# Hybrid attention layer on one core: the first norm's weights as one row spread by TensorE, and FoX value weights in row blocks

## The chip, the cores and the metric

The kernel runs on one NeuronCore of a Trainium2 chip. Its engines are TensorE (PE, with its weight loads listed apart as PEld), VectorE (DVE), ScalarE (ACT), GpSimd (POOL) and SyncE (SP), which issues most of the transfers. Each engine works through its own list of instructions in a fixed order. The metric is device time in microseconds (us) of one execution.

## The reference

The layer takes x (1024 tokens by 1024 channels, float32). It normalizes x, projects it, runs two attentions on the projections (a dilated sliding-window one and a forgetting one, "FoX"), merges them by sigmoid gates, adds the result to x, and then applies a second norm and a SwiGLU feed-forward part. The change lies in the first norm and in the FoX values:

```python
h = rms_norm(x, norm_mix_g[layer])           # x * rsqrt(mean(x*x) + 1e-6) * g
proj = h @ w_in[layer]
fox = proj[..., o2:o3].reshape(b, s, 3, N_FOX_HEADS, HEAD_DIM)
...
o_b = forgetting_attention(fox[:, :, 0], fox[:, :, 1], fox[:, :, 2],
                           jax.nn.log_sigmoid(f_logit))
```

`fox[:, :, 2]`, the values, are 512 columns of `proj`: 1024 tokens by 512, each a sum over the 1024 channels.

## The kernel before, in words

Every large product is made of three matmuls. `split` (lines 98 to 100) cuts a float32 operand into a rounded part `hi` (an ACT copy, line 99) and a rest `lo` (a DVE subtraction, line 100), and `mm3` (lines 102 to 105) adds hi·hi, hi·lo and lo·hi in one PSUM bank. So each weight tile costs ACT one pass and DVE one pass before TensorE can use it.

The kernel's first stage, the pool `foxv` from line 398 on, normalizes the eight blocks of 128 tokens and computes the FoX values. `norm_transpose` (lines 167 to 182) treats one block: ACT squares and sums it (line 171), `rstd` (lines 145 to 165) makes the factor with two small ACT operations (`t` on line 157 and `y` on line 158) and four small DVE ones, DVE multiplies by the factor and by the norm's weights `gain1` (line 173), and TensorE transposes the result `hn` in two groups of four 128x128 tiles (line 178), which `split` moves to `hT`. `values(i)` then multiplies block i of `hT` by the value weights `wv`.

What stands ahead of that is written out by hand. SP issues, in this order, the first block of x (`xt`, line 405), the norm's 1024 weights written to all 128 partitions (line 409), and then `wv` in four blocks of 128 columns with all 1024 rows (line 122, in `load_w`), the later blocks of x among them. TensorE starts with 20 matmuls of a constant tile `ones` whose result nobody reads (`dummies`, line 422), and later six more. The callback `between`, here `first_tokens`, puts the norm of block 0 between the splits of the first and second weight block, and the norm of block 1 between the second and third; `tc.issue_after(ins)` tells the scheduler to place what follows behind `ins` on the same engine, in order of issue only. Since a block of 128 columns serves only its own columns, `values` computes tokens of blocks 0 and 1 in two halves of 256 columns: the first half needs two weight blocks, and the second half the other two. From block 2 on it takes all 512 columns at once.

The rest of the layer follows in stages of its own: the dilated values, query and key projections, the two attentions, the gates, the output product and the feed-forward part. The scheduler chooses the order of instructions on each engine from the dependencies and from the `issue_after` edges.

Of the kernel before, what the change touches and what calls it, by code (L numbers as in the profile page):

```python
# [8 lines left out]
F32 = mybir.dt.float32  # L9
# [6 lines left out]
P = 128  # L16
D = 1024
# [30 lines left out]
def layer_kernel(  # L48
# [42 lines left out]
    def nm(s):  # L91
        uid[0] += 1
        return f"{s}_{uid[0]}"
# [11 lines left out]
        last_mm[0] = nc.tensor.matmul(psum, w.lo, m.hi, start=False, stop=stop)  # L105

    last_mm, last_hi, last_sq = [None], [None], [None]
    last_w, s12_hi = [None], [None]

    def load_w(src, kt, n, tag="w", bufs=2, pool=None, chunk=None, rpool=None, rbufs=2, shared=0, between=None):  # L110

        pool = pool or wpool
        row = -(-n // P) * P
        hi = pool.tile([P, kt, row], F32R, tag=tag + "h", name=nm("wh"), bufs=bufs)
        lo = pool.tile([P, kt, row], F32R, tag=tag + "l", name=nm("wl"), bufs=bufs)
        chunk = chunk or n
        for c0 in range(0, n, chunk):
            cs = slice(c0, min(n, c0 + chunk))
            own = rpool and c0 >= shared
            raw = (rpool if own else wpool).tile([P, kt, cs.stop - c0], F32, tag="wr", name=nm("wr"),  # L120
                                                 bufs=rbufs if own else 2)
            last_w[0] = nc.sync.dma_start(out=raw[:], in_=src[:, cs].rearrange("(k p) c -> p k c", p=P))
            if between and 0 < c0 <= 2 * chunk:
                between(c0 // chunk)

            with tc.issue_after((last_hi, last_sq)[c0 // chunk - 1][0].ins) if between and 0 < c0 <= 2 * chunk \
                    else ExitStack():
                split(hi[:, :, cs], lo[:, :, cs], raw[:])
        return Pair(hi, lo)


# [13 lines left out]
    def rstd(ss, by_sqrt):  # L145

        def tiny(n):
            return small.tile([P, 1], F32, tag=n, name=nm(n))

        y, t, v, r = tiny("y"), tiny("t"), tiny("v"), tiny("r")  # L150
        nc.vector.tensor_scalar(out=v[:], in0=ss[:], scalar1=1.0 / D, scalar2=EPS,
                                op0=ALU.mult, op1=ALU.add)
        if by_sqrt:
            nc.scalar.activation(out=t[:], in_=ss[:], func=AF.Sqrt, scale=1.0 / D, bias=epst[:])
            nc.vector.reciprocal(out=y[:], in_=t[:])
        else:
            nc.scalar.activation(out=t[:], in_=ss[:], func=AF.Ln, scale=1.0 / D, bias=epst[:])
            nc.scalar.activation(out=y[:], in_=t[:], func=AF.Exp, scale=-0.5)
        t2 = tiny("t2")
        nc.vector.tensor_scalar(out=t2[:], in0=y[:], scalar1=v[:, 0:1], scalar2=y[:, 0:1],  # L160
                                op0=ALU.mult, op1=ALU.mult)
        nc.vector.tensor_scalar(out=t2[:], in0=t2[:], scalar1=-0.5, scalar2=1.5,
                                op0=ALU.mult, op1=ALU.add)
        nc.vector.tensor_scalar(out=r[:], in0=y[:], scalar1=t2[:, 0:1], scalar2=None, op0=ALU.mult)
        return r

    def norm_transpose(xt, gain, hT, col, pool, by_sqrt, bufs=2):
# [2 lines left out]
        ss = small.tile([P, 1], F32, tag="ss", name=nm("ss"))  # L170
        last_sq[0] = nc.scalar.activation(out=hn[:], in_=xt, func=AF.Square, accum_out=ss[:])
        r = rstd(ss, by_sqrt)
        nc.vector.scalar_tensor_tensor(out=hn[:], in0=xt, scalar=r[:, 0:1], in1=gain[:],  # L173
                                       op0=ALU.mult, op1=ALU.mult)
        for k0 in range(0, KT, 4):
            pt = psf.tile([P, HALF], F32, tag="f", name=nm("pt"))
            for k in range(4):
# [220 lines left out]
    with pool_of("foxv", 2) as vpool:  # L398
# [7 lines left out]

        load_x()
        gain1 = vpool.tile([P, D], F32, tag="gain", name=nm("gain"), bufs=1)
        nc.sync.dma_start(out=gain1[:], in_=norm_mix_g.broadcast_to([P, D]))
        nc.gpsimd.memset(ones[:], 1.0)  # L410

        warm = pd()
# [7 lines left out]
        def dummies(n):  # L420
            for i in range(n):
                nc.tensor.matmul(warm[:, :P], ones[:], ones[:], start=True, stop=True)

        def first_tokens(n):
            if n == 1:
                load_x()
                norm_transpose(xts[0][:], gain1, hT[0], 0, vpool, False)
                dummies(6)
            else:
                with tc.issue_after(last_hi[0].ins):  # L430
                    norm_transpose(xts[1][:], gain1, hT[0], P, vpool, False)

        dummies(20)
        wv = load_w(w_in[:, FOX0 + 2 * FOX_W:FGT0], KT, FOX_W, tag="wv", bufs=1, pool=vpool,
                    chunk=P, rpool=vpool, rbufs=3, shared=2 * P, between=first_tokens)

        def values(i):
            hh, c = divmod(i * P, HALF)
            st = vpool.tile([P, FOX_W], F32, tag="vst", name=nm("vst"), bufs=2)
            n = 256 if i < 2 else FOX_W  # L440
            for c0 in range(0, FOX_W, n):
                pv = pd()
                for k in range(KT):
                    mm3(pv[:, :n], hT[hh][:, k, c:c + P], wv[:, k, c0:c0 + n], k == 0, k == KT - 1)
                nc.vector.tensor_copy(st[:, c0:c0 + n], pv[:, :n])
            nc.gpsimd.dma_start(out=vf_dram[i], in_=st[:])

        for i in range(NT):
# [893 lines left out]
```

## Time and profile before

| | |
|---|---|
| median of 3 runs | 1468.48 us (1467.93 to 1469.89) |
| the profiled execution | 1468.82 us, of which the span is 1467.1 us |
| busy share of the span: PE, PEld, DVE, ACT, POOL | 98%, 79%, 65%, 38%, 34% |
| PE busy in the first 20 us | 14.41 us |
| PE busy from 40 to 60 us | 20.00 us |

The span runs from the first to the last instruction that the profile counts; 1.7 us of the execution's own time lie around it. In the profile's rows a time stands at the start in us from the beginning of the span, then the duration, the engine, the line of the kernel, the operation, and output and input by the program's names. `[... <-X]` tells how long the engine was idle before the row and what ended that. A matmul's duration is modelled and overlaps the next one's, so the distance between two starts is what a matmul costs in a row of them.

### The profile page before, as it was taken

Reading aid. Unit: us, or ns where it says so; the run is one execution under the profiler, and the core shown is the slowest. Engines: PE = TensorE matmul, PEld = TensorE weight load, DVE = VectorE, ACT = ScalarE, POOL = GpSimd, SP = SyncE. Lnnn points to the kernel's source line nnn. Section 1 sums busy time; section 2 is a strip of 40 time slices with the busy share of each in tenths; the row PEclk is TensorE's granted clock in tenths of the full one; section 3 lists DMA queues with packets and bytes.
Section 4 is the critical chain, followed back from the end, with each engine's and each line's share of the span. In section 5 each row is a group of like instructions: output and inputs, shape, how many; then the busy total and the mean of one; then the engine's idle time right before and its main releaser. Section 6 shows DMA issues by size and latency. Waiting matters only on the chain. (4 is left out here: it accounts for less than half of the span.)

```text
span 1467.1 us, 18389 instructions
## 1 busy us (share of the span) xinstructions
PE 1441.3 (98%) x6876; PEld 1162.5 (79%) x6876; DVE 956.6 (65%) x1336; ACT 553.3 (38%) x824; POOL 504.1 (34%) x438
## 2 busy tenths in 40 slices
PE   8999999999999999999999999999999999999997
PEld 7898888877677776788887778888888887788886
DVE  6484654359889999846528865555556555876555
ACT  5333332236656423354315432223223323543333
POOL 1020444535533321110146166666666665000000
PEclk9999999999999999999999999999999999999999
DMA  7232454575543461265759312323233332986502
GB/s 231 72 101 79 144 166 124 139 212 130 129 122 102 168 206 36 80 233 170 293 201 367 106 58 80 107 93 104 98 108 108 107 103 88 384 287 210 164 29 86
DMA packets 165785, 213.58 MB, mean 146 GB/s; under 512 B 13760, under 2 KB 115136, under 8 KB 165440
## 3 DMA queue, kind: packets, MB, share of 16 engines
q1 hardware_dynamic: 129376, 119.06, 26.2%
q0 software_dynamic: 15344, 55.59, 10.4%
q10 hardware_dynamic: 20976, 37.76, 8.2%
q8 instruction: 54, 0.88, 0.3%
q14 instruction: 35, 0.29, 0.1%
HBM read 146.32 MB, written 66.06 MB: 145 GB/s over the span
## 5 line engine op out<-in xcount | busy, mean ns | idle before, releaser
L299 PE MATMUL pd<-hT_t,wh 128*128 128x512 f32 x856 | 265.0, 390 | 1.4 <-DVE sg L1037 0.6
L299 PE MATMUL pd<-tT,wh 128*128 128x512 f32 x768 | 235.1, 389 | 0.7 <-ACT wh L99 0.6
L100 DVE TENSOR_TENSOR wl<-wr,wh 128x1024 fp32r<-128x1024 f32 (+2 forms) x110 | 131.2, 1194 | 127.9 <-ACT wh L99 127.3
L99 ACT ACTIVATE wh<-wr 128x1024 fp32r<-128x1024 f32 (+2 forms) x110 | 95.4, 867 | 285.6 <-PE pd L299 166.2
L299 PEld LDWEIGHTS pd<-hT_t,wh 128*128 128x128 f32 x856 | 160.0, 188 | 37.8 <-DVE sg L1037 4.7
L299 PEld LDWEIGHTS pd<-tT,wh 128*128 128x128 f32 x768 | 144.0, 188 | 31.4 <-ACT wh L99 1.0
L299 PE MATMUL pd<-hT_t,wl 128*128 128x512 f32 x428 | 166.5, 389 | 0.0
L299 PE MATMUL pd<-tT,wl 128*128 128x512 f32 x384 | 147.6, 389 | 0.0
L105 PE MATMUL pf<-hT_t,wl 128*128 128x512 f32 x288 | 114.5, 398 | 0.0
L103 PE MATMUL pf<-hT_t,wh 128*128 128x512 f32 x288 | 114.1, 396 | 0.0
L104 PE MATMUL pf<-hT_t,wh 128*128 128x512 f32 x288 | 113.7, 395 | 0.0
L100 DVE TENSOR_TENSOR ol<-raw,oh 128x1024 fp32r<-128x1024 f32 x66 | 79.6, 1223 | 45.8 <-ACT oh L99 38.5
L99 ACT ACTIVATE wh<-s 128x1024 fp32r<-128x1024 f32 x58 | 61.4, 1060 | 118.3 <-POOL s L286 91.3
L285 POOL TENSOR_TENSOR s<-wr 128x512 f32<-128x512 f32 x29 | 60.4, 2084 | 123.9 <-DMA wr<-in_w_in_dram 71.0
L99 ACT ACTIVATE oh<-raw 128x1024 fp32r<-128x1024 f32 x66 | 69.2, 1060 | 87.4 <-PE pd L1257 66.8
L299 PEld LDWEIGHTS pd<-hT_t,wl 128*128 128x128 f32 x428 | 80.3, 188 | 16.9
L100 DVE TENSOR_TENSOR wl<-s,wh 128x1024 fp32r<-128x1024 f32 x58 | 72.2, 1246 | 32.3 <-ACT wh L99 32.3
L1257 PE MATMUL pd<-ol,oh 128*128 128x512 f32 x224 | 87.2, 390 | 1.7 <-DVE ol L100 1.7
L1257 PE MATMUL pd<-oh,ol 128*128 128x512 f32 x224 | 86.3, 389 | 0.0
L984 POOL TENSOR_TENSOR r<-r 128x512 f32<-128x512 f32 x32 | 44.2, 1391 | 120.7 <-DMA r<-in_w_ffn_down_dram 119.3
L299 PEld LDWEIGHTS pd<-tT,wl 128*128 128x128 f32 x384 | 72.1, 188 | 15.0
L1257 PE MATMUL pd<-oh 128*128 128x512 f32 x224 | 83.9, 389 | 0.0
(277 smaller groups left out, 3068.4 us busy)
## 6 DMA issues: line engine op xcount, KB each, us to landing
wr<-in_w_in_dram SPq DMA_DIRECT2D x46, 512.0 KB, 4.7
wr<-in_w_ffn_in_dram SPq DMA_DIRECT2D x44, 512.0 KB, 3.8
raw<-left_dram SPq DMA_DIRECT2D x56, 256.0 KB, 5.3
g_dram<-fst ACTq DMA_DIRECT2D x32, 256.0 KB, 2.5
land<-g_dram SPq DMA_DIRECT2D x16, 512.0 KB, 3.4
r<-in_w_ffn_down_dram SPq DMA_DIRECT2D x8, 1024.0 KB, 10.4
right_dram<-r POOLq DMA_DIRECT2D x8, 1024.0 KB, 6.2
left_dram<-f POOLq DMA_DIRECT2D x8, 1024.0 KB, 4.7
```

The lines of the kernel that those rows point to most:

```text
L99: last_hi[0] = nc.scalar.activation(out=hi, in_=src, func=AF.Copy)
L100: return nc.vector.tensor_tensor(out=lo, in0=src, in1=hi.bitcast(F32), op=ALU.subtract)
L103: nc.tensor.matmul(psum, w.hi, m.hi, start=start, stop=False)
L104: nc.tensor.matmul(psum, w.hi, m.lo, start=False, stop=False)
L105: last_mm[0] = nc.tensor.matmul(psum, w.lo, m.hi, start=False, stop=stop)
L285: nc.gpsimd.tensor_tensor(out=s12[:, :4], in0=u1, in1=u2, op=ALU.add)
L299: last_mm[0] = nc.tensor.matmul(bank[:], p, q, start=first and k == 0 and n == 0, stop=k == 3 and n == 2, skip_group_check=True)
L984: nc.gpsimd.tensor_tensor(out=out, in0=p, in1=q, op=ALU.subtract)
L1257: nc.tensor.matmul(bank[:], p, q, start=new and n == 0 and i == 0, stop=n == last and i == 2, skip_group_check=True)
```

## The change

The norm's weights now come as one row of 1024 numbers to partition 0, in place of a copy for each partition. TensorE spreads them: two matmuls multiply a row of ones by 512 weights each, ACT copies the first half from PSUM to `gain1`, and DVE the second half. The first norm is placed behind these two copies on ACT and on DVE.

The value weights are loaded and split in four blocks of 256 rows (two tiles of 128 channels) and all 512 columns, in place of four blocks of 128 columns. `values` therefore takes all 512 columns at once for every token block. The order of the first splits is told by hand: block 0 behind `y` (ACT) and `hn` (DVE) of the first norm, block 1 behind the last ACT copy of the first `hT`, block 2 behind the square of the second norm, and block 3 behind the ACT half of block 2's split.

```diff
-        nc.sync.dma_start(out=gain1[:], in_=norm_mix_g.broadcast_to([P, D]))
+        nc.sync.dma_start(out=gain1[0:1, :], in_=norm_mix_g)
...
         def first_tokens(n):
+            if n == 0:
+                with tc.issue_after(spread[0]), tc.issue_after(spread[1]):
+                    norm_transpose(xts[0][:], gain1, hT[0], 0, vpool, False)
+                first_hi.append(last_hi[0].ins)
+                dummies(6)
+                return last_y[0].ins, last_hn[0].ins
             if n == 1:
                 load_x()
-                norm_transpose(xts[0][:], gain1, hT[0], 0, vpool, False)
-                dummies(6)
-            else:
+                return first_hi
+            if n == 2:
                 with tc.issue_after(last_hi[0].ins):
                     norm_transpose(xts[1][:], gain1, hT[0], P, vpool, False)
+                return [last_sq[0].ins]
+            return [last_hi[0].ins]
 
         dummies(20)
-        wv = load_w(w_in[:, FOX0 + 2 * FOX_W:FGT0], KT, FOX_W, tag="wv", bufs=1, pool=vpool,
-                    chunk=P, rpool=vpool, rbufs=3, shared=2 * P, between=first_tokens)
+        spread, first_hi = [], []
+        for c in (slice(0, HALF), slice(HALF, D)):
+            pg = pd()
+            nc.tensor.matmul(pg[:], ones[0:1, :], gain1[0:1, c], start=True, stop=True)
+            if c.start == 0:
+                spread.append(nc.scalar.activation(out=gain1[:, c], in_=pg[:], func=AF.Copy).ins)
+            else:
+                spread.append(nc.vector.tensor_copy(gain1[:, c], pg[:]).ins)
+        wv = Pair(*[vpool.tile([P, KT, FOX_W], F32R, tag="wv" + n, name=nm("wv"), bufs=1) for n in "hl"])
+        for n in range(KT // 2):
+            raw = (vpool if n > 1 else wpool).tile([P, 2, FOX_W], F32, tag="wr", name=nm("wr"), bufs=2)
+            last_w[0] = nc.sync.dma_start(out=raw[:], in_=w_in[2 * n * P:2 * (n + 1) * P, FOX0 + 2 * FOX_W:FGT0].rearrange(
+                "(k p) c -> p k c", p=P))
+            with ExitStack() as behind:
+                for ins in first_tokens(n):
+                    behind.enter_context(tc.issue_after(ins))
+                split(wv.hi[:, 2 * n:2 * n + 2], wv.lo[:, 2 * n:2 * n + 2], raw[:])
 
         def values(i):
             hh, c = divmod(i * P, HALF)
             st = vpool.tile([P, FOX_W], F32, tag="vst", name=nm("vst"), bufs=2)
-            n = 256 if i < 2 else FOX_W
-            for c0 in range(0, FOX_W, n):
-                pv = pd()
-                for k in range(KT):
-                    mm3(pv[:, :n], hT[hh][:, k, c:c + P], wv[:, k, c0:c0 + n], k == 0, k == KT - 1)
-                nc.vector.tensor_copy(st[:, c0:c0 + n], pv[:, :n])
+            pv = pd()
+            for k in range(KT):
+                mm3(pv[:], hT[hh][:, k, c:c + P], wv[:, k], k == 0, k == KT - 1)
+            nc.vector.tensor_copy(st[:], pv[:])
             nc.gpsimd.dma_start(out=vf_dram[i], in_=st[:])
```

The order of the instructions shows where the new ones stand. Line numbers in the rows of the changed kernel are its own (line 409 is the dummies, 158 the square, 165 the transposes). The first place is the start of TensorE's list; `pd_110` is the bank of the dummies, and `pt_161` and `pt_168` are the transposed halves of token block 0. Before:

```order
L422 MATMUL pd_110<-ones 128x128 x23
L178 MATMUL pt_161<-ident,hn_146 128x128 x4
L178 MATMUL pt_168<-ident,hn_146 128x128 x4
L422 MATMUL pd_110<-ones 128x128 x3
L103 MATMUL pd_225<-wh_136,hT_t 128x256
L104 MATMUL pd_225<-wl_137,hT_t 128x256
```

The same place in TensorE's list of the changed kernel:

```order
L409 MATMUL pd_110<-ones 128x128 x20
L431 MATMUL pd_136<-gain_107,ones 128x512
L431 MATMUL pd_139<-gain_107,ones 128x512
L409 MATMUL pd_110<-ones 128x128 x6
L165 MATMUL pt_161<-ident,hn_146 128x128 x4
L165 MATMUL pt_168<-ident,hn_146 128x128 x4
L103 MATMUL pd_231<-wv_142,hT_t 128x512
```

The two spreading matmuls stand behind the first 20 dummies, and all 26 dummies stand ahead of the transposes.

The second place is the start of ACT's list. `xt_105`, `xt_144` and `xt_220` are the token blocks 0, 1 and 2, and `wh_136<-wr_...` are the ACT halves of the four weight splits. Before:

```order
L171 ACTIVATE hn_146,ss_147<-xt_105 128x1024
L157 ACTIVATE t_150<-ss_147,epst 128x1
L158 ACTIVATE y_149<-t_150 128x1
L99 ACTIVATE wh_136<-wr_138 128x8x128
L99 ACTIVATE hT_t<-pt_161 128x4x128
L99 ACTIVATE hT_t<-pt_168 128x4x128
L99 ACTIVATE wh_136<-wr_142 128x8x128
L171 ACTIVATE hn_185,ss_186<-xt_144 128x1024
L99 ACTIVATE wh_136<-wr_183 128x8x128
L99 ACTIVATE wh_136<-wr_216 128x8x128
L157 ACTIVATE t_189<-ss_186,epst 128x1
L171 ACTIVATE hn_280,ss_281<-xt_220 128x1024
```

The same place in ACT's list of the changed kernel, where the token blocks 1 and 2 are called `xt_185` and `xt_226`:

```order
L433 ACTIVATE gain_107<-pd_136 128x512
L158 ACTIVATE hn_146,ss_147<-xt_105 128x1024
L144 ACTIVATE t_150<-ss_147,epst 128x1
L145 ACTIVATE y_149<-t_150 128x1
L99 ACTIVATE wv_142<-wr_144 128x1024
L99 ACTIVATE hT_t<-pt_161 128x4x128
L99 ACTIVATE hT_t<-pt_168 128x4x128
L99 ACTIVATE wv_142<-wr_183 128x1024
L158 ACTIVATE hn_191,ss_192<-xt_185 128x1024
L99 ACTIVATE wv_142<-wr_189 128x1024
L99 ACTIVATE wv_142<-wr_222 128x1024
L158 ACTIVATE hn_260,ss_261<-xt_226 128x1024
```

ACT's first instruction is now the copy of a spreading matmul's result, and the square of token block 0 stands behind it. The first small operation of block 1 (`t_189` before) no longer stands ahead of the square of block 2; it follows behind these rows.

The third place is DVE's list at the norms of blocks 1 and 2, where `vst` is the copy of finished values and `hT_t<-pt_200` (before) and `hT_t<-pt_206` (now) the DVE half of block 1's split after the transposes. Before:

```order
L164 TENSOR_SCALAR r_191<-y_188,t_25_195 128x1
L162 TENSOR_SCALAR t_41_290<-t_41_290 128x1
L173 SCALAR_TENSOR_TENSOR hn_185<-xt_144,r_191,gain_107 128x1024
L164 TENSOR_SCALAR r_286<-y_283,t_41_290 128x1
L445 COPY vst_224<-pd_225 128x256
L173 SCALAR_TENSOR_TENSOR hn_280<-xt_220,r_286,gain_107 128x1024
L445 COPY vst_224<-pd_251 128x256
L100 TENSOR_TENSOR hT_t<-pt_200,hT_t 128x4x128
L100 TENSOR_TENSOR hT_t<-pt_207,hT_t 128x4x128
```

The same place in the changed kernel:

```order
L151 TENSOR_SCALAR r_197<-y_194,t_27_201 128x1
L151 TENSOR_SCALAR r_266<-y_263,t_42_270 128x1
L160 SCALAR_TENSOR_TENSOR hn_191<-xt_185,r_197,gain_107 128x1024
L160 SCALAR_TENSOR_TENSOR hn_260<-xt_226,r_266,gain_107 128x1024
L452 COPY vst_230<-pd_231 128x512
L100 TENSOR_TENSOR hT_t<-pt_206,hT_t 128x4x128
L100 TENSOR_TENSOR hT_t<-pt_213,hT_t 128x4x128
```

Both factors (`r_`) now stand ahead of block 1's multiplication, and the values' copy, once two halves around block 2's multiplication, is one piece behind it. Block 1's split stands behind all of these in both kernels.

More of the change, by code (lines that the diff above doesn't have):

```diff
@@ L107, in layer_kernel, with load_w @@
     last_mm, last_hi, last_sq = [None], [None], [None]
[L108 to L128, printed above, removed]
+    last_w, s12_hi, last_y, last_hn = [None], [None], [None], [None]
+    def load_w(src, kt, n, tag="w", pool=None):
+        hi, lo = [(pool or wpool).tile([P, kt, -(-n // P) * P], F32R, tag=tag + h, name=nm("w" + h), bufs=2) for h in "hl"]
+        raw = wpool.tile([P, kt, n], F32, tag="wr", name=nm("wr"), bufs=2)
+        last_w[0] = nc.sync.dma_start(out=raw[:], in_=src.rearrange("(k p) c -> p k c", p=P))
+        split(hi[:], lo[:], raw[:])
         return Pair(hi, lo)
@@ L157, in rstd @@
             nc.scalar.activation(out=t[:], in_=ss[:], func=AF.Ln, scale=1.0 / D, bias=epst[:])
-            nc.scalar.activation(out=y[:], in_=t[:], func=AF.Exp, scale=-0.5)
+            last_y[0] = nc.scalar.activation(out=y[:], in_=t[:], func=AF.Exp, scale=-0.5)
         t2 = tiny("t2")
@@ L172, in norm_transpose @@
         r = rstd(ss, by_sqrt)
-        nc.vector.scalar_tensor_tensor(out=hn[:], in0=xt, scalar=r[:, 0:1], in1=gain[:],
-                                       op0=ALU.mult, op1=ALU.mult)
+        last_hn[0] = nc.vector.scalar_tensor_tensor(out=hn[:], in0=xt, scalar=r[:, 0:1], in1=gain[:],
+                                                    op0=ALU.mult, op1=ALU.mult)
         for k0 in range(0, KT, 4):
```

## The prediction

> **What bounds the kernel now.** The page comes first: TensorE is busy 98% of the span, no other engine above 79%.
>
> ```profile
> span 1467.1 us, 18389 instructions
> PE 1441.3 (98%) x6876; PEld 1162.5 (79%) x6876; DVE 956.6 (65%) x1336; ACT 553.3 (38%) x824; POOL 504.1 (34%) x438
> ```
>
> The change touches only the start, so the busy times by stretches come next (PE first after the stretch's length, the granted clock third from the end).
>
> ```profile
> 0.00:20.00 20.00, 14.41 (x95) 13.52 (x96) 9.77 (x19) 11.26 (x19) 3.48 (x13) 0.98 0.99 271
> 20.00:40.00 20.00, 19.75 (x127) 17.85 (x127) 14.94 (x30) 8.89 (x20) 1.83 (x3) 0.94 0.48 155
> 40.00:60.00 20.00, 20.00 (x101) 16.67 (x101) 13.19 (x23) 8.74 (x18) 1.63 (x3) 1.00 0.33 103
> ```
>
> TensorE sits idle for 5.6 us in the first 20 and hardly after that. So the question is when it begins the third token block's values, the first matmuls that both kernels have in the same form: what that moment moves, the end moves too, since TensorE paces what follows. The timeline gives the way there.
>
> ```profile
> 1.39 7.33 PE L422 MATMUL pd<-ones 128*128 128x128 f32 x46 [1.39 <-POOL ones L410]
> 4.67 1.06 ACT L171 ACTIVATE hn<-xt 128x1024 f32<-128x1024 f32 x1 [2.60 <-DMA xt<-in_x_dram]
> 7.23 1.28 DVE L173 SCALAR_TENSOR_TENSOR hn<-xt,r,gain 128x1024 f32<-128x1024 f32 x1
> 8.15 1.06 ACT L99 ACTIVATE wh<-wr 128x1024 fp32r<-128x1024 f32 x1 [1.71 <-DMA wr<-in_w_in_dram]
> 8.66 1.06 PE L178 MATMUL pt<-ident,hn 128*128 128x128 f32 x8
> 9.32 1.09 ACT L99 ACTIVATE hT_t<-pt 128x512 fp32r<-128x512 f32 x2
> 11.11 1.06 ACT L99 ACTIVATE wh<-wr 128x1024 fp32r<-128x1024 f32 x1 [0.70 <-DMA wr<-in_w_in_dram]
> 12.21 0.38 PE L103 MATMUL pd<-wh,hT_t 128*128 128x256 f32 x1 [1.82 <-ACT wh L99]
> 14.23 1.06 ACT L99 ACTIVATE wh<-wr 128x1024 fp32r<-128x1024 f32 x1 [0.61 <-DMA wr<-in_w_in_dram]
> 16.00 1.06 ACT L99 ACTIVATE wh<-wr 128x1024 fp32r<-128x1024 f32 x1 [0.71 <-DMA wr<-in_w_in_dram]
> 22.72 1.04 PE L178 MATMUL pt<-ident,hn 128*128 128x128 f32 x8
> 25.15 0.36 PE L105 MATMUL pd<-wh,hT_t 128*128 128x256 f32 x1
> 30.93 0.40 PE L103 MATMUL pd<-wh,hT_t 128*128 128x512 f32 x1
> 31.17 0.40 PE L104 MATMUL pd<-wl,hT_t 128*128 128x512 f32 x1
> 31.40 0.39 PE L105 MATMUL pd<-wh,hT_t 128*128 128x512 f32 x1
> ```
>
> The square of token block 0 starts when x lands (4.67). The values of block 0 do not start with the first norm: its `hT` is there from 10.4 (9.32 + 1.09), and TensorE waits until 12.21 for the second weight block, whose split waited for its landing until 11.11. The transposes of block 1 follow at 22.72, the first matmul that needs the `lo` half of its `hT` runs at 25.15, and block 2's values begin at 30.93. From 25.15 on TensorE does not stop. The start is thus bound by landings first, and then by the splits.
>
> **The change part by part.** *The spread weights, the largest term.* ACT's first instruction is now the copy of the first spreading matmul, and the square of block 0 is queued behind it; so is all of ACT's list. On TensorE that matmul is queued behind 20 dummies. When do these end, and what does a float32 matmul of 512 columns cost? A dummy leaves two records:
>
> ```profile
> 1.38:7.80 6.42, 6.41 (x40) 6.41 (x41) 1.37 (x5) 2.34 (x5) 2.46 (x4) 1.00 0.91 275
> L422 PE MATMUL pd<-ones x52: 275/275/579, 1.4 to 10.1; 128*128 128x128 f32 x52
> L714 PE MATMUL pd<-mx,ones x32: 592/592/643, 346.0 to 519.4; 128*64 128x512 f32 x32
> 345.98 1.08 PE L714 MATMUL pd<-mx,ones 128*64 128x512 f32 x4 [0.58 <-DVE mx L700]
> ```
>
> The 40th record has begun by 7.80, so the 20 dummies are through by 7.9. Going from 128 to 512 columns adds 592 - 275 = 317 ns, 0.83 ns a column, so a record of 512 columns holds TensorE for 0.42 us. (The four records on line 714 took 1.08 us; they write two partition halves and may run in pairs, and if they do not, one costs 0.25. I take 0.42, from the durations, and keep 0.25 as the lower end.) Two records: the first result is there at 7.9 + 0.42 + 0.59 = 8.9. These rows give the durations of the engines' passes:
>
> ```profile
> L171 ACT ACTIVATE hn<-xt 128x1024 f32<-128x1024 f32 x5 | 5.3, 1056 | 3.0 <-DMA xt<-in_x_dram 2.9
> L99 ACT ACTIVATE hT_t<-pt 128x512 fp32r<-128x512 f32 x6 | 3.3, 592 | 6.3 <-PE pt L178 6.2
> L157 ACT ACTIVATE t<-ss,epst 128x1 f32<-128x1 f32 x5 | 1.5, 291 | 0.2
> L100 DVE TENSOR_TENSOR wl<-wr,wh 128x1024 fp32r<-128x1024 f32 x4 | 4.9, 1226 | 3.3 <-ACT wh L99 3.3
> L173 DVE SCALAR_TENSOR_TENSOR hn<-xt,r,gain 128x1024 f32<-128x1024 f32 x4 | 5.1, 1283 | 0.1
> L100 DVE TENSOR_TENSOR hT_t<-pt,hT_t 128x512 fp32r<-128x512 f32 x6 | 4.0, 687 | 1.3 <-ACT hT_t L99 1.3
> ```
>
> ACT's copy of 512 columns out of PSUM is of the size of the `hT` copy, 0.59, so the square starts at 9.5 and not at 4.67: 4.8 later. The second spread and DVE's copy (like the 0.69 of the `hT` rest) end near 10.4, before DVE's first operation on the norm, and cost nothing.
>
> *The weight blocks.* The 512 KB of the copied weights no longer go ahead of the blocks, and rows of a block are four times as long. This is worth nothing here: with the square at 9.5, ACT asks for the four blocks not before 10.6 (9.5 + 1.06), 15.2, 17.4 and 18.5 (below), against landings until now at 8.15, 11.11, 14.23 and 16.00, so each could come 2.4 us later than before and still be in time. What falls away is every wait for a landing; what is late next is the chain on ACT and DVE itself.
>
> *The chain.* Block 0's multiplication moves from 7.23 to 12.0 and ends at 13.3, the transposes run from 13.5, and ACT's two `hT` copies from 14.1 to 15.2. Then ACT works through its list without a wait: the second weight block until 16.3 (1.06), the square of block 1 until 17.4, the third and fourth weight blocks until 19.5, the square of block 2 until 20.6 with 0.1 for reading its sum, and two small `t` of 0.29 each until 21.3, where `y` of block 1 starts. DVE's rest of the fourth weight block ends at 21.0 (18.5 + 2 x 1.23), so TensorE has six matmuls left at that moment and is through block 0 at about 22.3, with 512 columns 0.23 us apart. Then it waits for block 1:
>
> ```profile
> 18.39 0.19 ACT L158 ACTIVATE y<-t 128x1 f32<-128x1 f32 x1
> 19.51 1.29 DVE L173 SCALAR_TENSOR_TENSOR hn<-xt,r,gain 128x1024 f32<-128x1024 f32 x1
> 20.72 0.21 DVE L164 TENSOR_SCALAR r<-y,t 128x1 f32<-128x1 f32 x1
> 27.50 0.28 PE L103 MATMUL pd<-wh,hT_t 128*128 128x256 f32 x1
> 27.62 0.60 PE L178 MATMUL pt<-ident,hn 128*128 128x128 f32 x4
> 27.97 0.36 PE L105 MATMUL pd<-wh,hT_t 128*128 128x256 f32 x1
> ```
>
> From `y` to the multiplication passed 1.1 us; now block 2's `r` stands in between too (0.21), so block 1 is multiplied from 22.6 to 23.9. On DVE block 2's multiplication (to 25.2), the values' copy (0.69, to 25.9) and the first rest of `hT` (0.69, to 26.6) follow. TensorE transposes block 1 from 24.0 meanwhile, and its first matmul on that rest runs at 26.65, against 25.15 before.
>
> *The wider matmuls.* Before, 48 matmuls of 256 columns made a block's values; they start 0.12 apart (27.50 to 27.62), 5.8 us a block. Now it is 24 of 512, 0.23 apart, 5.5 us. In block 0 this is hidden under the waits for splits. In block 1, 22 are left at 26.65: 22 x 0.23 = 5.1, and four transposes in between take 0.35 more than the matmul distance (27.50 to 27.97, less 0.12). Block 2 begins at 26.65 + 5.1 + 0.35 = 32.1 against 30.93: **1.2 us later**. Later blocks and stages have the same matmuls.
>
> *The clock.* Part of the time before was lost to it (PE's busy time, then the granted clock):
>
> ```profile
> 8.83:12.24 3.41, 1.59 (x15) 1.00 1.11 276
> 15.66:19.07 3.41, 1.91 (x14) 1.00 1.09 347
> 19.07:22.48 3.41, 3.41 (x19) 0.51 1.14 310
> ```
>
> After 3.41 us with TensorE half idle, 3.41 us were granted at half clock, with 16 matmuls 0.21 apart in place of 0.12, 1.4 us in all. The stretch from 8.83, less busy still, was followed by full clock, so these rows give no plain threshold. Now TensorE is half idle from 10.9 (7.9, two spreads of 0.85 and six dummies of 0.21) to 22.3 and nearly idle from there to 26.65; half clock before 24 would be hidden by the wait, later it would not. I take none in the sum, and keep 3.41 / 2 = 1.7 as the upper end.
>
> [...]
>
> Sum: 1468.82 us of the profiled execution + 1.2 = 1470.0. That execution lies 0.34 above the median of the runs; on the median, 1468.48 + 1.2 = **1469.7 us**. What a measurement of this kernel can tell from no change is about 0.2%, 2.9 us.
>
> **The rivals.** *Half clock on block 1 (slower).* [...] If a half-clock window begins within some 0.3 us of 26.65, the 1.7 comes on top, and with 0.3 for the handovers between engines that I left out the time is 1469.7 + 2.0 = 1471.7. For it speaks the half clock at 19.07, against it the stretch from 8.83 and that a window must fall just there. 23 in 100, with other lateness of that size.
>
> *The square is not held (faster).* If the first spread were through by the landing of x, the chain would run 4.8 earlier, and 1.2 later would become 3.6 earlier: 1464.9. It decides at 4.1: the first result must leave TensorE by then (4.67 - 0.59). Against it stands TensorE's list with the 20 dummies ahead, to 7.9. 6 in 100; with gains of other kinds, such as the end of the landing waits counting for more than I think, 10.
>
> *The spread is cheap and the chain tighter.* With 0.25 a record and 0.7 us less in ACT's list than its durations add up to, the delay shrinks to 0.2: 1468.7. 20 in 100; it lies within the forecast's bound.
>
> **How the numbers follow.** The forecast, 1469.7, with what lies within 2.9 us of before, has 67 in 100 (20 of them for the third rival), slower by over 0.2% 23, faster by over 0.2% 10. The range reaches down past the third rival by the spread of the runs of before (0.5 below and 1.4 above their median) toward the faster case, 1467.2, and up past the half-clock case to 1472.4.
>
> **What would show it.** In the changed kernel's timeline: the first spreading matmul at 7.9, ACT's copy from 8.9, the square of block 0 at 9.5; no wait of ACT for a weight landing; block 1's multiplication near 22.6; TensorE idle from 22.3 to 24; block 2's values at 32.1. A square near 4.7, a wait for a weight landing, or block 2's values before 30 would make the forecast wrong, as would a shift at block 2's start that does not reach the end.

## The result, and the profile after

The changed kernel takes 1474.02 us (median of 13 runs, 1470.06 to 1479.63), the kernel before in the same comparison 1468.7 (13 runs). The ratio is 1.0037 with a 95% interval of 1.0025 to 1.0049: slower by 5.4 us by the ratio, where 1.2 were forecast. The profiled execution took 1472.62 us. The first lines of its page:

```profile
span 1470.8 us, 18303 instructions
PE 1443.2 (98%) x6832; PEld 1159.8 (79%) x6832; DVE 954.8 (65%) x1335; ACT 552.2 (38%) x825; POOL 506.4 (34%) x438
```

Its first two stretches of 20 us, with the columns of before:

```profile
0.00:20.00 20.00, 15.71 (x77) 12.47 (x77) 7.31 (x12) 9.23 (x15) 3.48 (x13) 1.00 0.88 267
20.00:40.00 20.00, 18.55 (x93) 14.72 (x93) 15.89 (x35) 9.96 (x26) 1.57 (x3) 1.00 0.41 130
```

TensorE has 44 records fewer than before (6832 for 6876): 24 matmuls less in each of two blocks, four records more for the spread. This number turns out to matter. The granted-clock column stands at 1.00 in both stretches, but the dummies show slower matmuls at the very start. From 1.5 to 4.9 us each of the two kernels has 16 of their records, 0.21 us each. In the next 3.4 us before has 30 (first row) and the changed kernel 22 (second):

```profile
4.90:8.30 3.40, 3.40 (x30) 1.00 1.14 301
4.90:8.30 3.40, 3.40 (x22) 1.00 1.01 350
```

So in this execution the dummies ran slowly for longer, and the same 20 ended later.

The timeline of the start answers to the rows of before:

```profile
1.39 7.52 PE L409 MATMUL pd<-ones 128*128 128x128 f32 x40 [1.39 <-POOL ones L397]
8.84 1.98 PE L431 MATMUL pd<-gain,ones 1*128 1x512 f32 x4
10.00 0.60 ACT L433 ACTIVATE gain<-pd 128x512 f32<-128x512 f32 x1 [7.92 <-PE pd L431]
10.50 1.05 ACT L158 ACTIVATE hn<-xt 128x1024 f32<-128x1024 f32 x1
13.04 1.28 DVE L160 SCALAR_TENSOR_TENSOR hn<-xt,r,gain 128x1024 f32<-128x1024 f32 x1
14.47 1.06 PE L165 MATMUL pt<-ident,hn 128*128 128x128 f32 x8 [2.11 <-DVE hn L160]
16.10 1.06 ACT L99 ACTIVATE wv<-wr 128x1024 fp32r<-128x1024 f32 x1
17.05 1.06 ACT L158 ACTIVATE hn<-xt 128x1024 f32<-128x1024 f32 x1
21.40 0.34 ACT L145 ACTIVATE y<-t 128x1 f32<-128x1 f32 x2
22.44 2.47 DVE L160 SCALAR_TENSOR_TENSOR hn<-xt,r,gain 128x1024 f32<-128x1024 f32 x2
23.86 1.07 PE L165 MATMUL pt<-ident,hn 128*128 128x128 f32 x8 [0.62 <-DVE hn L160]
26.58 0.48 PE L105 MATMUL pd<-wv,hT_t 128*128 128x512 f32 x1
32.18 0.39 PE L103 MATMUL pd<-wv,hT_t 128*128 128x512 f32 x1
```

The square stands behind the copy of the first spread (10.00, then 10.50), and every step of block 0 is about 1 us later than forecast. ACT makes this good: its passes of 1.06 start 0.95 apart (16.10, then 17.05), and `y` of block 1 begins at 21.40, forecast at 21.3. Block 2's values begin at 32.18 against 30.93: the start costs 1.25.

To see where the rest comes from, rows of DVE and ACT that both traces have were lined up and their times subtracted. The changed kernel lies 1.3 behind from 150 to 600 us, 0.9 behind at 1200, and 3.7 behind from 1330 to the end. So 2.8 us arise in one place, at the start of the feed-forward's down product. There the second split's rest (`ol`, line 100) is written where the last `a` was kept, which a store is still reading. DVE's and TensorE's rows of before there:

```profile
1252.97 1.23 DVE L100 TENSOR_TENSOR ol<-raw,oh 128x1024 fp32r<-128x1024 f32 x1 [5.17 <-DMA raw<-left_dram]
1254.25 0.50 PE L1257 MATMUL pd<-ol,oh 128*128 128x512 f32 x1 [1.74 <-DVE ol L100]
```

The first row names another transfer as what ended the wait, but the store, issued at 1245.20, lands 7.6 later, at 1252.8, just ahead of it.

The DMA queues of before from the issue of the store (`a_dram<-a`) to its landing: packets, MB and share of the 16 engines; for the store the us from issue to landing.

```profile
q1 hardware_dynamic: 1007, 1.84, 76.8%
q0 software_dynamic: 209, 0.79, 25.0%
a_dram<-a POOLq DMA_DIRECT2D x1, 512.0 KB, 7.6
```

The same two rows of the changed kernel:

```profile
1255.12 1.22 DVE L100 TENSOR_TENSOR ol<-raw,oh 128x1024 fp32r<-128x1024 f32 x1 [6.42 <-DMA a_dram<-a]
1256.40 0.69 PE L1264 MATMUL pd<-ol,oh 128*128 128x512 f32 x1 [2.98 <-DVE ol L100]
```

Its queues from that issue to that landing:

```profile
q1 hardware_dynamic: 1103, 2.02, 67.0%
q0 software_dynamic: 291, 1.09, 29.6%
q8 instruction: 1, 0.02, 0.6%
a_dram<-a POOLq DMA_DIRECT2D x1, 512.0 KB, 8.8
```

Its TensorE in the stretch of the wait and in the next one: busy time, granted clock, DMA share, GB/s.

```profile
1253.10:1256.50 3.40, 0.41 (x3) 1.00 1.04 416
1256.50:1259.90 3.40, 3.40 (x9) 0.51 1.03 404
```

The store lands 8.8 us after its issue in place of 7.6, TensorE waits 1.24 longer, and after this stretch with 0.41 us of work it gets 3.4 us of half clock (0.51), which costs about half of it, 1.7. Together that is about the 2.8. One packet is new in the changed kernel's rows: one of queue q8, whose kind is "instruction".

### The profile page after: what moved, and what is told of

It reads as the page before. It is cut to its first block, busy times and chain, and to the rows that moved or that the text cites. A ratio compares the mean times of both kernels' runs of the same rounds, so it can differ in the third digit from the quotient of the medians.

```text
span 1470.8 us, 18303 instructions
## 1 busy us (share of the span) xinstructions
PE 1443.2 (98%) x6832; PEld 1159.8 (79%) x6832; DVE 954.8 (65%) x1335; ACT 552.2 (38%) x825; POOL 506.4 (34%) x438
## 4 chain that ended last, share of the span: by engine, by line
PE 83%; DVE 10%; POOL 2%; issue 2%; ACT 2%; DMA 1%; ACTq 0%; DVEq 0%; POOLq 0%
PE pd L286 33%; PE pd L1264 10%; PE pd L103 6%; PE pd L105 6%; PE pd L104 6%; PE pf L105 3%; PE pf L104 3%; PE pf L103 3%; DVE wl L100 2%; PE pd L718 1%; PE pd L184 1%; PE pd L187 1%; PE pd L183 1%; PE pd L667 1%; PE pd L668 1%
## 5 line engine op out<-in xcount | busy, mean ns | idle before, releaser
L100 DVE TENSOR_TENSOR wl<-wr,wh 128x1024 fp32r<-128x1024 f32 (+2 forms) x106 | 126.3, 1193 | 126.7 <-ACT wh L99 126.0
L99 ACT ACTIVATE wh<-wr 128x1024 fp32r<-128x1024 f32 (+2 forms) x106 | 91.1, 860 | 279.9 <-PE pd L286 165.5
```

Of the source, the lines that this page charges most:

```text
L99: last_hi[0] = nc.scalar.activation(out=hi, in_=src, func=AF.Copy)
L100: return nc.vector.tensor_tensor(out=lo, in0=src, in1=hi.bitcast(F32), op=ALU.subtract)
```

## The experiments

Each ran beside runs of the kernel before, on the same chip; between groups of experiments the chip differed, so the ratios are what compares. The first theory was one of order. Beyond the start, the scheduler orders a few splits and copies at the down product otherwise than before. The orders that matter below are that of before, that of the changed kernel, and that of e3.

**e1: the order alone.**

```diff
         for i in range(NT):
             load_x()
+            if i == 2:
+                dummies(6)
```

> The kernel before with six more matmuls of the constant tile on TensorE, behind the values of token block 1, so that block 2's values begin some 1.2 us later, as in the changed kernel; nothing else of the change is in it. In the changed kernel's profile block 2's values begin 1.25 us later than before, but the span is 3.7 us longer, and 2.8 of that arise at the start of the feed-forward's down product, where TensorE waits 2.98 us in place of 1.74 for a split on DVE and a half-clock window follows; the median of the runs is even 5.3 longer. Theory A (order): any delay of TensorE's start makes the scheduler order the splits at the start of the down product otherwise, as in the changed kernel, and that order costs some 4 us: this kernel has that order, so it takes 1473 to 1475, ratio 1.003 to 1.004. Theory B (delay only): a later start costs its own length, and the rest is chance of landings and clock windows: 1469 to 1471, ratio 1.0005 to 1.0015. Theory C (the changed kernel's own start costs more in the timed runs than in the profile): as B.

Measured: 1470.28 us against 1468.47, ratio 1.0006 [0.9998, 1.0015]. The six dummies did not delay block 2; they ran in an earlier wait, behind the three that stood there:

```profile
9.46 2.17 PE L422 MATMUL pd<-ones 128*128 128x128 f32 x18
```

So the start moved by only 0.1, but the order at the down product is word for word that of the changed kernel, and TensorE waits 1.7 there as before. Theory A falls: that order is not what costs 4 us.

**e2: the spread alone** (the column blocks stay; the spread and its edges as in the change).

> Only the first part of the change: the norm's weights as one row, spread by two matmuls behind the 20 dummies; the weight blocks stay columns. The square of block 0 starts near 10 to 10.5 in place of 4.67, behind the first weight block's split, and block 2's values begin 1 to 3 us later than before. The order at the start of the down product is that of the kernel before. Theory A (order): the delay alone counts, 1469.5 to 1471.5, ratio 1.0007 to 1.002, and the start of the down product looks as before. Theory B: the same, with the wait at the down product changed or not by chance. Theory C: the held square costs more in timed runs than in the profile: 1473 or more, ratio over 1.003.

Measured: 1478.34 us, ratio 1.0061 [1.0048, 1.0073]. The start misses all theories: the values are 7.9 later.

```profile
10.06 0.60 ACT L440 ACTIVATE gain<-pd 128x512 f32<-128x512 f32 x1 [2.49 <-PE pd L438]
14.51 1.06 ACT L99 ACTIVATE wh<-wr 128x1024 fp32r<-128x1024 f32 x1 [2.82 <-DMA wr<-in_w_in_dram]
15.48 0.28 ACT L157 ACTIVATE t<-ss,epst 128x1 f32<-128x1 f32 x1
18.92 1.94 PE L178 MATMUL pt<-ident,hn 128*128 128x128 f32 x8 [6.50 <-DVE hn L173]
```

Its clock in the stretches after that wait:

```profile
20.21:23.62 3.41, 1.23 (x5) 0.50 0.32 125
23.62:27.03 3.41, 3.28 (x15) 0.50 0.59 158
```

ACT's list puts the second weight split (14.51) ahead of the small `t`, so the norm waits for a landing, TensorE waits 6.50 for the norm, and then runs at half clock until 27. Its down product is as before, but the trace loses 2.7 more near 800 us, the place that e5 shows below. The time lies where theory C put it (1473 or more), though not for theory C's reason. So this run says what the spread costs without the told order of splits, not what it costs in the change.

**e3: the row blocks alone.**

```diff
-        nc.sync.dma_start(out=gain1[0:1, :], in_=norm_mix_g)
+        nc.sync.dma_start(out=gain1[:], in_=norm_mix_g.broadcast_to([P, D]))
...
-        for c in (slice(0, HALF), slice(HALF, D)):
-            pg = pd()
...
```

> Only the second part of the change: weight blocks of 256 rows with the order of the first splits told, and the norm's weights copied to all partitions as before. The square starts at the landing of x, near 4.7 to 6, and block 2's values begin near 29, 2 us earlier than before. The order at the start of the down product is a third one, neither that before nor that of the changed kernel. Theory A (order): the time can lie on either side by what that order costs, 1466 to 1472. Theory B (delay only): 1466 to 1467.5, ratio 0.998 to 0.999. Theory C: as B.

Measured: 1474.22 us, ratio 1.0035 [1.0024, 1.0046]. The start is 3.0 earlier, as expected, and the kernel is slower all the same, beyond every expectation: its trace loses 1.8 near 310 us and 5.6 at the down product, with a wait of TensorE of 4.67 there.

**e4: the spread behind 6 dummies.**

```diff
-        dummies(20)
+        dummies(6)
...
+        dummies(14)
```

> The changed kernel with six dummies ahead of the spreading matmuls and fourteen behind, in place of twenty ahead. The first spread is through near 5 in place of 9, the square of block 0 starts at 5.5 to 6.5, and block 2's values begin near 28 to 29, 2 to 3 us earlier than before and 3 to 4 earlier than in the changed kernel. Its order at the start of the down product is also not that of the changed kernel. Theory B and C (the start alone): 1465.5 to 1467.5, ratio 0.998 to 0.999. Theory A (order): up to 4 us more if its order has the same wait, 1466 to 1471.

Measured: 1475.47 us, ratio 1.0041 [1.0029, 1.0053]. The scheduler put 14 of the 20 ahead, the square began at 8.23 and the start came 0.3 earlier than before; the trace loses 2.7 near 300 us and 5.1 at the down product. All theories missed.

By now the kernels with row blocks lose at the down product, and those with column blocks don't. The trace's DMA records name a difference. Queue q8, whose kind is "instruction", moves packets of 16 KB, one every 27 us on average (54 in 1467.1 us). The page of before has

```profile
q8 instruction: 54, 0.88, 0.3%
```

and it is taken to be TensorE's. 6876 matmuls and as many weight loads make 254.7 of both together for each of the 54 packets. The eleventh packet begins at 272.7 us in before and at 285.1 in the changed kernel, after 1349 matmuls in the one and 1355 in the other. And the packets' times move with the number of TensorE's records (the table below). No run here shows TensorE itself waiting for a packet; one takes 0.9 to 1.5 us in the trace of before. 44 records fewer delay the later packets: before, one begins 8.5 us ahead of the store's issue, in the changed kernel 5.7 behind it, while the store is under way.

**e5, e6: the changed kernel with records added** (22 and 8 matmuls of 16 columns in TensorE's wait for the first norm).

```diff
+        def short(n):
+            for i in range(n):
+                nc.tensor.matmul(warm[:, :16], ones[:], ones[:, :16], start=True, stop=True)
...
                 dummies(6)
+                short(22)
```

> The changed kernel with 22 more matmuls of 16 columns of the constant tile in TensorE's wait ahead of block 0's transposes: 44 records, as many as the row blocks save, so that TensorE's program is as long as before from there on. In the order of the down product it equals the changed kernel. The profiles so far: TensorE's program comes in transfers of 16 KB, one every 28 us or so; in the kernels with row blocks one of them falls 5 to 7 us behind the issue of the last store of a, at the start of the down product, and that store lands 8.7 to 9.2 us after its issue in place of 7.6; in the kernels with column blocks the transfer falls 8.5 us ahead of the store. Theory D (program transfer): the 44 records put the transfer back ahead of the store, the store lands in 7.6, TensorE waits 1.7 in place of 3.0 for the split, no half clock follows, and the loss at the down product goes; the start alone is left: 1469.5 to 1471, ratio 1.0007 to 1.002. Theory E (the row blocks do it in some other way, by their shape or their place in memory, or it is chance): 1473 to 1475.5, ratio 1.003 to 1.0045.

> As the run with 44 records more, with 8 such matmuls, 16 records: the transfer moves about 4 to 5 us earlier and still falls between the issue of the store and its landing. Theory D: it still costs, in all 1472 to 1475, ratio 1.002 to 1.0045, but less or more by where it falls. Theory E: as the changed kernel, 1473 to 1475.5. It tells what the added matmuls do by themselves.

Measured: 1475.18 us, ratio 1.0041 [1.0027, 1.0054], and 1471.82 us, ratio 1.0017 [1.0008, 1.0026]. The first missed, since a short matmul is not short:

```profile
11.44 4.89 PE L413 MATMUL pd<-ones 128*128 128x16 f32 x42
```

0.116 us a record, as much as with 128 columns (0.121, 18 in 2.17 in e1); 44 need 5.1 where the wait has 2.1, and the start is 3.8 later than before, not 1.3. At the down product the packet is back ahead of the store, which lands in 8.1; TensorE still waits 2.2. This trace, of e5's longest run, loses 2.7 more at a third place, near 800 us. The same row of before and of e5:

```profile
799.09 1.26 PE L178 MATMUL pt<-ident,hn 128*128 128x128 f32 x8 [0.71 <-DVE hT_t L100]
804.64 1.97 PE L165 MATMUL pt<-ident,hn 128*128 128x128 f32 x8 [2.78 <-DVE hT_t L100]
```

The wait is 2.78 in place of 0.71, and the eight records behind it take 1.97 in place of 1.26. e5 has as many records as before, and e2 four more, so fewer records are not what costs time at this place; why the split on DVE is late there was not tested.

In e6 the 16 records fit the wait (start 1.0 later), the transfer falls 1.1 behind the store's issue and, against expectation, costs nothing there: the store lands in 7.6, TensorE waits 1.77. And the median of e6 is 2.2 us below that of the changed kernel, with about the same start.

**e7: the kernel before with 44 records fewer.**

```diff
-                nc.tensor.matmul(warm[:, :P], ones[:], ones[:], start=True, stop=True)
+                nc.tensor.matmul(warm[:], ones[:], ones[:].unsqueeze(1).broadcast_to([P, 4, P]), start=True, stop=True)
...
-                dummies(6)
...
-        dummies(20)
+        dummies(4)
```

> The kernel before, with four matmuls of 512 columns in place of its 26 dummies of 128: 8 records in place of 52, so 44 fewer, as the row blocks make it, and about the same time of TensorE ahead of the first transposes. The start stays bound by the landings, within 0.5 us or, if the clock comes later, 1.5. The order at the down product is that of the changed kernel. Theory D: the transfer falls 5 to 7 us behind the store's issue, the store lands near 8.8, and the down product loses 2.8 to 5 us: 1471 to 1474, ratio 1.002 to 1.0035. Theory E: 1468 to 1470, ratio 0.9997 to 1.001.

Measured: 1474.57 us against 1468.98, ratio 1.0032 [1.0019, 1.0046]. No spread, no row blocks, a start 1.6 earlier than before in the profile, and yet as slow as the change. The store lands in 9.1, TensorE waits 3.20. Theory E (1468 to 1470) is out; the ratio lies in theory D's range.

**e8: the row blocks alone with 44 records added** (`short(22)`, as in e5; 4 fewer than before in all).

> The row blocks alone, with the norm's weights copied to all partitions, and 22 short matmuls more, 44 records. The row blocks alone began later blocks 3.0 us earlier than before and lost 5.6 at the down product. Theory D: the loss goes, the gain of the start is left, less up to 1 us for the short matmuls: 1465.5 to 1468, ratio 0.998 to 0.9997. Theory E: 1472.5 to 1475, ratio 1.0027 to 1.0045.

Measured: 1471.91 us, ratio 1.0016 [1.0005, 1.0028]: 2.3 faster than e3, not the 6 to 9 expected. The store lands in 7.7 and TensorE waits 1.87, but half clock follows all the same (0.58 granted from 1253.4 to 1256.8), and the short matmuls took back 1.6 of the start's gain.

**The second place.** The traces of e4 and e7 also lose 2.7 and 4.4 near 300 us. There SP loads the next weights (`wr`, issued at 286.65 before) while POOL loads the attention's operands. ACT's row at that landing, of before:

```profile
292.92 1.06 ACT L99 ACTIVATE wh<-wr 128x1024 fp32r<-128x1024 f32 x1 [6.88 <-DMA wr<-in_w_in_dram]
```

The same row of e7:

```profile
295.61 1.06 ACT L99 ACTIVATE wh<-wr 128x1024 fp32r<-128x1024 f32 x1 [11.18 <-DMA wr<-in_w_in_dram]
```

Its queues from 280 to 288 us; before has the same stretch without a packet of q8:

```profile
q0 software_dynamic: 451, 1.51, 80.9%
q8 instruction: 1, 0.02, 0.7%
q1 hardware_dynamic: 18, 0.01, 0.6%
```

The changed kernel's profile has 8.40 there, just short of making TensorE wait.

**e9, e10, e11: the store's wait taken off the second split** (in the changed kernel, in that before, and in the row blocks alone). All operand tiles move by one buffer group; the fifth split waits for the store instead.

```diff
+        first_xr = [fpool.tile([P, D], F32, tag="xf", name=nm("xr"), bufs=3)]
...
-            xr = fpool.tile([P, D], F32, tag="xf", name=nm("xr"), bufs=3)
+            xr = first_xr.pop() if first_xr else fpool.tile([P, D], F32, tag="xf", name=nm("xr"), bufs=3)
```

> The changed kernel with the first xr tile set aside at the start of the down product's pool, so that all its operand tiles lie one buffer group further on in memory. The second split's rest no longer lies where the last a is stored from, and does not wait for that store; the fifth does, some 8 us later in the work. Nothing else moves on any engine, and TensorE's program is as long as in the changed kernel. Theory F (the store's wait, with the half clock that follows it, is what the changed kernel loses beyond its start): the wait of 2.98 at the second split falls below 1, the half-clock window behind it goes, 1468 to 1470.5, ratio 0.9995 to 1.0012, about 1.3 to 2 above the kernel before with the same edit. Theory G (the timed runs lose it elsewhere, at the start, near 300 or near 800 us): 1471.5 or more, 4 to 6 above the kernel before with the same edit.

> The kernel before with the same edit: its wait of 1.74 for the second split goes or shrinks below 1. Both theories: 1466.5 to 1468.5, ratio 0.9985 to 1.0.

> The row blocks alone, with the norm's weights copied to all partitions, and the same edit. Its start gains 3.0, and its loss of 5.6 at the down product goes under theory F, with the 1.7 of the kernel before as well: 1463.5 to 1466.5, ratio 0.9965 to 0.9985, the fastest so far. Theory G: 1468 to 1473.

Measured: 1471.94 us, ratio 1.0018 [1.0005, 1.0031]; 1469.05, ratio 0.9999 [0.9988, 1.0010]; 1470.12, ratio 1.0008 [0.9995, 1.0021]. The edit helps the kernels with the late transfer by 2 to 4 us and the kernel before by nothing. It does not take the wait away: the copies of `acc` on DVE are then late, and TensorE waits 1.1, 1.7 and 2.7 for those. Theory F's ranges for e9 and e11 were too low, since the second place stayed; both times lie where theory G put them, which has the loss elsewhere. The profile of e9 shows it at its worst:

```profile
301.55 1.06 ACT L99 ACTIVATE wh<-wr 128x1024 fp32r<-128x1024 f32 x1 [14.20 <-DMA wr<-in_w_in_dram]
302.66 0.79 PE L103 MATMUL pf<-hT_t,wh 128*128 128x512 f32 x1 [5.12 <-ACT wh L99]
```

Its TensorE in the stretch behind the wait:

```profile
304.00:308.00 4.00, 4.00 (x11) 0.52 1.02 325
```

A wait of 5.12 and half clock behind it: this trace loses 8.2 us there. Of the runs of e9 six took 1468.6 to 1470.4 us and six 1473.5 to 1477.1; the profiled one is the slowest of these.

**e12, e13: the row blocks alone with 16 and 24 records added** (`short(8)`, `short(12)`; 32 and 24 fewer than before in all, four more than the expectations count). Otherwise as e8.

> The row blocks alone, with the norm's weights copied to all partitions, and 8 short matmuls more, 16 records, 28 fewer than before. With 28 fewer the program transfers fell harmlessly at both places (280 us, ahead of the weights' load by 7.6, and 1.1 behind the store's issue). 44 short records took 5.0 us in the other run of the row blocks, so 16 take 1.8, of which the waits of block 0 and 1 hide most. Theory D, with both places: the weights at the attention's start land within 7.5 us of their issue, the store within 7.7, and what is left is the start's gain of 2 to 3: 1466.5 to 1469, ratio 0.998 to 1.0, below the row blocks alone (1474.2) by 5 to 7. Rival (the loss hangs on the row blocks, and 44 records cured it by their delay): 1472 or more.

> The row blocks alone with 12 short matmuls more, 24 records, 20 fewer than before. The scheduler then orders the start of the down product exactly as in the kernel before, which it did not with 8. Transfer and order are then both harmless: the weights at the attention's start land within 7.5 us, TensorE waits 1.7 to 1.9 at the down product, and the start's gain of 2 to 3, less up to 1 for the 2.7 us of short matmuls, reaches the end: 1465.5 to 1468, ratio 0.998 to 0.9995. If the order costs nothing (the wait of 4.0 with 16 records came from the landing alone): as with 16 records, 1469 to 1471. If the start's gain never reaches the end: 1468.5 or more.

Measured: 1469.71 us, ratio 1.0008 [0.9999, 1.0017], and 1466.97 us, ratio 0.9982 [0.9973, 0.9991]. e12 has the order and the start of e3, and its packet comes 7.6 ahead of the weights; its median is 4.5 below e3's, and by the two ratios it gains 4.0. So the row blocks are not to blame. It is still a little above its expected range, and it still waits at the down product, where the order of e3 stands:

```profile
1251.77 0.50 PE L1261 MATMUL pd<-ol,oh 128*128 128x512 f32 x1 [4.02 <-DVE ol L100]
```

e13 has the order of before (a wait of 2.58 in its profile, which is of its slowest run) and is faster than both kernels, as expected. So a kernel with the row blocks can be faster than before; where its shorter runs gain it no trace shows.

**All profiles in one table.** Records of TensorE against before; start: how much later rows lie at 150 to 220 us; the packet of q8: how long ahead of the weights' issue it began; ACT's wait for these weights; the packet against the store's issue; the store's landing; TensorE's wait at the down product (in brackets: for `acc`).

| kernel | records | start | packet ahead of weights | wait for weights | packet after store's issue | landing | wait | ratio |
|---|---|---|---|---|---|---|---|---|
| before | 0 | 0 | 14.0 | 6.9 | -8.5 | 7.6 | 1.7 | 1 |
| e1 | +12 | 0.1 | 14.9 | 7.0 | -9.3 | 7.6 | 1.7 | 1.0006 |
| e2 | +4 | 7.9 | 14.4 | 7.4 | -8.9 | 7.7 | 1.9 | 1.0061 |
| e5 | 0 | 3.8 | 14.1 | 7.3 | -9.1 | 8.1 | 2.2 | 1.0041 |
| e8 | -4 | -1.4 | 13.8 | 6.9 | -8.7 | 7.7 | 1.9 | 1.0016 |
| e10 | 0 | -1.3 | 14.3 | 6.5 | -8.5 | 8.2 | (1.7) | 0.9999 |
| e13 | -24 | -1.3 | 7.6 | 6.8 | 0.0 | 8.5 | 2.6 | 0.9982 |
| e6 | -28 | 1.0 | 7.6 | 7.2 | 1.1 | 7.6 | 1.8 | 1.0017 |
| e12 | -32 | -2.9 | 7.6 | 6.7 | 2.0 | 8.1 | 4.0 | 1.0008 |
| changed | -44 | 1.3 | 2.8 | 8.4 | 5.7 | 8.8 | 3.0 | 1.0037 |
| e4 | -44 | -0.3 | 3.0 | 10.8 | 5.4 | 9.0 | 5.0 | 1.0041 |
| e7 | -44 | -1.6 | 2.9 | 11.2 | 5.9 | 9.1 | 3.2 | 1.0032 |
| e9 | -44 | 1.4 | 3.3 | 14.2 | 5.5 | 8.9 | (1.1) | 1.0018 |
| e3 | -48 | -3.0 | 3.4 | 9.6 | 6.5 | 8.7 | 4.7 | 1.0035 |
| e11 | -48 | -2.6 | 3.3 | 13.8 | 6.5 | 7.5 | (2.7) | 1.0008 |

The weights split cleanly: 6.5 to 7.4 in nine profiles, 8.4 to 14.2 in the six whose packet began 2.8 to 3.4 ahead. The store's landings split less surely: 7.6 to 8.5 against 8.7 to 9.1, with e11's 7.5 on the wrong side, and 8.1 and 8.2 in e5 and e10, whose packet is long past. Each row is one execution. Those of e6, e8 and e10 lie 2 to 3 us below the medians of their kernels (1469.60, 1468.82 and 1466.29); those of e2, e5, e9 and e13 are the longest of theirs.

## Why the prediction was wrong

**The start** was right in mechanism: the square is held behind the spread, and the chain on ACT and DVE behind it. In the profile it was right in size too, but part of that is luck, since two errors cancel: block 2's values were forecast at 32.1 and began at 32.18. The square was 1.0 later than forecast (10.50 for 9.5). The end of the dummies, 7.9, had been read from one execution; the spread began at 8.84 here, near 8.1 in e5 and at 8.58 in e6, and a record of the spread took 0.50 in place of 0.42. ACT in turn was 0.9 quicker than forecast from the `hT` copies to `y` (6.3 us for 7.2), mostly since the forecast added up durations where the passes start 0.95 apart. So TensorE waited 0.62 ahead of block 1, not 1.7.

In the timed runs e6, which has the changed kernel's start (1.0 later in its own profile) and no late landing there, is 0.0017 slower than before, 2.5 us [1.2, 3.8]. Its profile, of its shortest run, is only 0.8 slower than that of before. What the other runs of e6 lose, and whether at the start, no trace shows. One candidate is the clock: the half-clock window of before at 19.07 fell on work and cost 1.4, and in e10, with the same start, it came earlier (0.50 from 14 to 17, 0.83 in the us after) and the values began 1.3 earlier. Against such a start the change is 2.5 later; but the profiled run of before lies at the median of its runs, so this is not shown.

**The waits for landings** went as forecast; ACT has none left in the start. **The wider matmuls** were costed at their time alone. There lies **the failed step**: "Later blocks and stages have the same matmuls", and from it "what that moment moves, the end moves too". The matmuls are the same, but TensorE has 44 records fewer in front of them, and the q8 packets of 16 KB come at other moments of the later stages: 2.8 ahead of the weights' issue for 14.0 before, and 5.7 behind the store's issue for 8.5 ahead of it. Two transfers have little slack there: the store lands just ahead of the split that waits for it (1252.8 and 1252.97 in before), and in e3 a wait of 9.6 for the weights made TensorE wait 0.5. In the changed kernel's profile block 2 begins 1.25 later and the end comes 3.7 later; the difference, with 2.8 of it at the down product, stands in no term of the sum. e7 makes the same 44 records fewer without the change and loses 4.7 us [2.8, 6.8]; e10 and e13 begin about as early as e7 and don't lose this. e3 and e12 differ by 16 records, with the same start and the same order at the down product, and by about 4 us. So the number of records costs time in the later stages. e5, which was to test this in the changed kernel itself, doesn't tell, since its start came 3.8 later. How much of the 5.4 is the records' share is an estimate: 2.9, if all of e6's 2.5 is the start.

**How the packet delays them** is not shown, and that it does so at the store is less sure than at the weights. In the trace of before the weights' transfer has packets of 512 bytes, POOL's loads beside it have packets of 4096, and a q8 packet takes 0.9 to 1.5 us. Against that, the wait for the weights is 1.5 to 7.3 us longer in the six profiles with a packet close ahead, so the packet's own time does not account for that alone. The trace doesn't name the engine of a packet; why the wait came to 8.40 in one execution and to 14.20 in another is open.

**The rivals.** Half clock on block 1 did not come in the profile (block 1's matmuls start 0.23 apart, as at full clock before), though a half-clock window came elsewhere, at 1256.5, behind a wait that was not foreseen. The square was held, so the faster case was out. The spread was not cheap: four records took 1.98. But the third rival's other half came true: the chain was tighter, by 0.9.

**What stays open.** The timed runs have no trace, and the changed kernel's profile is faster than its median (1472.62 and 1474.02); that their spread (1470 to 1480) comes from the second place is likely by e9's two groups and not shown. e8 has its packets where before has them and starts 1.4 earlier, and yet is slower by 0.0016, 2.4 us. Its profile (1468.82) ends level with that of before: the start's gain of 1.4 is about what the half clock at the down product takes (an estimate: half of some 3 us), and what the longer runs lose stands in no trace. Between e8 and e13 lie 5 us, though both start alike in their profiles; the 20 records and the order differ, and no run tells them apart. What e3's order costs rests on e12 against e13, which differ by 8 records as well.

## What to carry to other kernels

Here 44 records fewer on TensorE moved the "instruction" packet at the attention's start from 14.0 to 2.8 us ahead of the weights' issue, some 250 us behind the change. Where a change alters the number of instructions on the busiest engine and a profile shows a transfer with little slack, look at these packets beside it before and after. When a change costs or gains in a stage that it doesn't touch, line up rows of both traces by stage before explaining anything, and try the same kernel with a few dead instructions more: here 24 records, and the order that came with them, turned a loss of 5 us (e3) into a gain of 2.7 (e13), while 44 did not (e8).

## What the runs showed of the hardware

A float32 matmul of 16 columns took 0.113 (e8) to 0.116 us (e5) a record, one of 128 columns 0.121 (e1, 18 in 2.17). Waits of TensorE of 1.87 (e8), 2.58 (e13) and 2.98 us (the changed kernel) were followed by half clock: 0.58 granted from 1253.4 to 1256.8 in e8, 0.50 from 1256 to 1259 in e13 and 0.51 from 1256.5 to 1259.9 in the changed kernel. Waits of 1.74 (before), of 1.77 (e6) and, ahead of the transposes at 14.47 in the changed kernel, of 2.11 were not, so these rows give no plain threshold. From 1.5 to 4.9 us of the span 16 dummy records started in 3.4 us, and in the next 3.4 us 30 in the profile of before and 22 in that of the changed kernel, with 1.00 in the granted-clock column all along: the first matmuls were slow, for a time that differed between the two. A 16 KB packet of q8 took 0.9 to 1.5 us in the trace of before. In the six profiles where one began 2.8 to 3.4 us ahead of a load of 512 KB, the wait for that load was longer than before by 1.5 to 7.3 us (8.40 to 14.20 against 6.88).
